# Order and pacing of two expert tables in a fused transformer kernel: where the second table begins, and how four lists of numbers share the side work

## The chip, the cores and the metric

The kernel runs on one core of a Trainium2 chip. Its engines work side by side, each through its own list of instructions in order: TensorE (PE, matmuls), VectorE (DVE), ScalarE (ACT), GpSimd (POOL) and SyncE (SP); the last three also issue DMAs, which 16 DMA engines share. The metric is the time of one execution in microseconds (us): 4077.38 us as the median of three runs (4074.62 to 4083.49).

## The reference, cut to what matters

Two transformer blocks over 512 tokens of width 1024. All that the change touches is one layer of the first block, a product-key expert layer with 16384 experts, 8 heads and the 16 best experts of each head:

```
s    = einsum('thsd,hsnd->thsn', q, sub_keys)      # scores of 2 x 128 sub-keys
sv, si = top_k(s, 16)                              # per half, then the best 16 of the sums
top, pos = top_k(sv0 + sv1, 16);  e = index of the expert;  g = softmax(top)
act  = gelu(einsum('thkd,td->thk', u_tab[e], x))   # first table, 16384 x 1024
out  = einsum('thk,thkd->td', g * act, v_tab[e])   # second table, 16384 x 1024
```

Everything is float32. The other layers (attention, a state-space mixer, cross attention, gated feed-forward layers) stay as they are.

## The kernel before, in words

A float32 product is made of three matmuls of the faster fp32r type: each operand is split into a high and a low part (`halves`: ACT writes `whi` at L119, DVE writes `wlo` at L120), and `mm3` (L167 to L169) adds high x high, high x low and low x high in PSUM. Weights come by SP in pieces of 1 MB into three buffers `wraw`, the split parts lie in three pairs of 128x1024, so the split can be at most one and a half pieces ahead of PE.

The expert layer (`experts`) splits the tokens. **384 tokens** are done densely: all 16384 experts are evaluated, and a sparse matrix of gates picks what counts.
- First table: 64 units (`unit`, L1245, counted from 1 here), each of 256 experts: 1 MB of weights, 48 matmuls with 384 columns, two Gelus (L1252) into `at`, which ACT writes to DRAM (`act_dram`, L1258). Such a group of results is called spilled.
- Gates: `select` finds the 16 best per token (DVE), `gates` (L1184) builds for 16 tokens at a time a 128x128 matrix per token out of two one-hot tiles `ga` and `gb` (DVE and ACT), multiplies them on PE (L1190), and ACT copies the result transposed into `st` (L1191) and stores it to `gate_dram` (L1218, L1223). 96 steps of four tokens each. A row of four tokens is a step of the generator `side`.
- Second table: 16 groups of 1024 experts. `weigh` (L1278) reads a group's gates `gt` (POOL, L1283) and activations `ac` (POOL, L1330), multiplies them (`wt`, L1287) and splits the product on ACT and DVE (L158, L159) into tiles `x` or `w`. `combine` (L1294) multiplies it with four pieces of the second table, each 1 MB and 48 matmuls with 384 columns. `weigh` of a group is written ahead of `combine` of the group before it.

**128 tokens** are done by gathering (`gathered`, L997): for each of 128 slots POOL gathers a row of the first table for every token (an indirect DMA of 128 rows of 4 KB, L1005) and DVE takes its dot product (L1010); 18 slots later POOL gathers a row of the second table and DVE adds it to `accg` (L1021). These 256 steps are called rows below. A row is made to wait on PE's last matmul of a unit or piece two (DVE) or four (POOL) before it (`paced`), so that it doesn't run ahead. What is left of them is issued at the start of the last group (L1298), since the sum is needed after three of its four pieces.

Numbers share the side work out. After each unit `due` grows by `DUE` = 6.5, and steps of `side` are issued until their costs have used it up; a gate step costs `GCOST` = 2.0, and steps of `gates` and of the next `select` alternate. `some(n)` adds n to a credit and issues one row per whole credit: 1.5 per unit of the first table once the rows may begin (from the seventh unit), 2 per unit that is evaluated in the second part, 2.75 per piece of the second table (`RATE`). The loop over units (L1255) goes on while side work is left, at most to 64; here side work ends with unit 62 and the count is rounded up to 64. So `first` = 16: all 16 groups are spilled and read back, in the order 0 to 15. A scheduler then orders each engine's list by when operands should be ready, so instructions can stand before others that were written earlier.

The tiles of the first part (`pa`, `pg`) give their memory to those of the second (`pb`): the first writer there waits for all that used it.

Of the kernel before, what the change touches and what calls it, by code (L numbers as in the profile page):

```python
# [21 lines left out]
P = 128  # L22
# [11 lines left out]
         + [(f"ffn_g{l}{i}", 8) for l in range(2) for i in range(2)]  # L34
         + [("mixer0_g", 8), ("mixer1_g", 8), ("subln_g", 1), ("mla_g_q", 4), ("mla_g_kv", 2), ("mla_g_qn", 1), ("mla_g_kn", 1)])
LAG, DUE = 2, 6.5
GCOST = 2.0
AHEAD, OUT_AT, EARLY = 0, 40, 2
PRE0, FILL0 = 2, 12
ON_POOL = (2, 3, 4, 5, 6, 7)  # L40
GATHERED = 128
PACE, PACE_D, AHEAD_G = 2, 4, 1
RATE = (1.5, 2, 2.75)
OHB, UGB = 1, 6
ULAG = 1
FIRST, STEP = (6, 3, 3), (1, 1, 1)
# [6 lines left out]
class Kern:  # L53
# [929 lines left out]
    def experts(self, ctx):  # L983
# [71 lines left out]
        with tc.tile_pool(name="pa", bufs=1) as sp_, ExitStack() as es:  # L1055
# [21 lines left out]
            x, xt = [], []  # L1077
# [106 lines left out]
            def gates(tt):  # L1184
# [8 lines left out]
                for tb in range(max(tt * P - G, 0) // TG, (tt * P + P - G) // TG):  # L1193
                    st = self.t(ap, [P, P, TG], "st", bufs=2)
                    for t0 in range(0, TG, 4):
                        t = tb * TG + t0
                        a = self.t(ap, [P, 4, P], "ga", bufs=LAG + 2)
                        four = lambda n: picks[n][:, t:t + 4, None].to_broadcast([P, 4, P])
                        rows4 = iota[:, None, :].to_broadcast([P, 4, P])

                        if t0 // 4 % 4 != 3:
                            nc.vector.tensor_tensor(a, rows4, four(0), op=ALU.is_equal)
                            for i in range(4):
                                nc.scalar.activation(a[:, i, :], a[:, i, :], AF.Copy, scale=picks[2][:, t + i:t + i + 1])
                        else:
                            for i in range(4):
                                nc.scalar.activation(a[:, i, :], iota, AF.Abs, bias=picks[0][:, t + i:t + i + 1], scale=-1.0)
                            for i in range(4):
                                nc.scalar.activation(a[:, i, :], a[:, i, :], AF.Relu, bias=picks[2][:, t + i:t + i + 1],
                                                     scale=picks[3][:, t + i:t + i + 1])  # L1210
                        bs = self.t(ap, [P, 4, P], "gb", bufs=LAG + 1)
                        nc.vector.tensor_tensor(bs, rows4, four(1), op=ALU.is_equal)
                        late.append((st, t0, a, bs, tb))
                        if len(late) > LAG:
                            z = late.pop(0)
                            finish(*z[:4])
                            if z[1] == TG - 4:
                                nc.scalar.dma_start(gate_d[z[4]], z[0].rearrange("p i t -> p (i t)"))  # L1218
                        yield GCOST
                for z in late:  # L1220
                    finish(*z[:4])
                    if z[1] == TG - 4:
# [29 lines left out]
                    nc.scalar.activation(out[:, i, :], ps, AF.Gelu)  # L1252

            work, due, b = side(), 0.0, 0
            while b < 64 and (b < 60 or work is not None or b % 4):  # L1255
                at = self.t(ap, [P, 2, N], "at", bufs=2)
                unit(b, at)
                nc.scalar.dma_start(act_d[b], at.rearrange("p a t -> p (a t)"))  # L1258
# [6 lines left out]
                    else:  # L1265
                        due -= c
                if room:
                    some(RATE[0])
            for _ in work or ():
                pass  # L1270
        first = b // 4
        with tc.tile_pool(name="pb", bufs=2) as ap:
# [45 lines left out]
                            if dh == 1:  # L1318
                                self.done(m)

            order, W = [*range(first, 16), *range(first)], None
            for i, c in enumerate(order):
                ac = [self.t(ap, [P, 2, 2, N], "ac", bufs=3) for _ in range(2)]
                if c >= first:
                    for b in range(4):
                        unit(c * 4 + b, ac[b // 2][:, b % 2])
                        some(RATE[1])
                else:
                    for b in range(2):
                        nc.gpsimd.dma_start(ac[b].rearrange("p b a t -> p b (a t)"), act_d[c * 4 + 2 * b:c * 4 + 2 * b + 2].rearrange("b j c -> j b c"))  # L1330
                W2 = weigh(c, lambda b: ac[b // 4][:, b % 4 // 2, b % 2, :], *((ap, "w") if i % 2 else (self.xp, "x")))
                if W is not None:
                    combine(order[i - 1], W, i == 1, False)
                W = W2
# [554 lines left out]
```

## Time and profile before

| | before |
|---|---|
| median of three runs | 4077.38 us |
| the profiled execution | 4081.56 us, span 4079.8 us |
| PE busy | 3915.7 us (96%) |
| DVE busy | 2464.4 us (60%) |
| ACT busy | 1733.6 us (42%) |
| POOL busy | 742.2 us (18%) |
| units of the first table | 618.1 (end of the first) to 1279.7 us |
| last Gelu to first matmul of the second table | 1279.7 to 1296.0 us |
| second table | 1296.0 to 1901.0 us |

The profile is one execution. PE is busy nearly all the time, so time is to be had only where it idles or runs at a low clock; a share over the whole span hides that. The views used below: busy time by stretch, with the clock that was granted to TensorE (1.00 is 2.4 GHz, 0.50 is 1.2 GHz) and the share of the DMA engines; instructions in order of time; totals of waits; groups of instructions by line; and the DMA queues.

### The profile page before, as it was taken

What the parts mean: (1) busy time and instruction counts of PE and PEld (TensorE: products, weight loads), DVE (VectorE), ACT (ScalarE), POOL (GpSimd) and SP (SyncE); (2) the same over time, 40 slices, a digit from 0 to 9 for tenths busy, and PEclk for the clock granted to TensorE, in tenths of its full rate; (3) what the DMA queues carried; (4) which work ended last, traced back from release to release, by engine and by line L of the source; (5) the groups of instructions that cost most, each with busy time, mean ns of one, the idle gap of its engine ahead of it and who ended that gap; (6) DMA issues with size and microseconds to landing.
All of it is one profiled execution on the core that took longest, in us unless ns stands there. A gap on an engine that the chain in (4) does not pass through costs nothing.

```text
span 4079.8 us, 52099 instructions
## 1 busy us (share of the span) xinstructions
PE 3915.7 (96%) x20105; PEld 3436.6 (84%) x20105; DVE 2464.4 (60%) x4683; ACT 1733.6 (42%) x3040; POOL 742.2 (18%) x706
## 2 busy tenths in 40 slices
PE   7999999999997898999999999999999999999999
PEld 6878789899987898898888778888888888888887
DVE  7666449987655787876434665743444446665443
ACT  3445434567684333333223356522332236654222
POOL 7401101122212455553000200100010001010000
PEclk8989999999998999999999999999999999999999
DMA  4204126677867999994232310323232222121222
GB/s 136 78 27 145 62 83 213 235 261 260 273 232 248 355 361 351 347 352 166 88 104 88 105 63 32 104 87 105 87 104 88 103 91 73 42 102 64 98 102 80
DMA packets 130907, 611.42 MB, mean 150 GB/s; under 512 B 22417, under 2 KB 25665, under 8 KB 90337
## 3 DMA queue, kind: packets, MB, share of 16 engines
q1 hardware_dynamic: 55296, 362.96, 25.5%
q0 software_dynamic: 48960, 187.31, 13.2%
q10 hardware_dynamic: 26400, 57.80, 3.9%
q8 instruction: 158, 2.59, 0.3%
q14 instruction: 93, 0.75, 0.1%
HBM read 553.49 MB, written 54.53 MB: 149 GB/s over the span
## 4 chain that ended last, share of the span: by engine, by line
PE 52%; DVE 5%; DMA 3%; ACT 1%; issue 1%; POOL 1%; ACTq 0%; DVEq 0%; POOLq 0%
PE ps_ffn L168 12%; PE ps_ffn L169 12%; PE ps_ffn L167 12%; DMA gt_peer<-gate_dram 2%; PE ps_mixer L168 2%; PE ps_mixer L167 2%; PE ps_mixer L169 2%; PE ps_xm L167 1%; PE ps_xm L169 1%; PE ps_xm L168 1%; PE ps_peer L169 1%; PE ps_peer L167 1%; PE ps_peer L168 1%; PE ps_mixer L1696 1%; PE ps_mixer L1549 1%
## 5 line engine op out<-in xcount | busy, mean ns | idle before, releaser
L119 ACT ACTIVATE whi_ffn<-wraw_ffn 128x1024 fp32r<-128x1024 f32 (+2 forms) x304 | 278.7, 944 | 923.6 <-PE ps_ffn L168 920.3
L167 PE MATMUL ps_peer<-xh_peer,whi_peer 128*128 128x384 f32 (+1 forms) x1664 | 582.0, 350 | 37.4 <-ACT whi_peer L119 18.1
L169 PE MATMUL ps_peer<-xh_peer,wlo_peer 128*128 128x384 f32 (+1 forms) x1664 | 576.4, 348 | 42.0 <-DVE wlo_peer L120 41.9
L168 PE MATMUL ps_peer<-xl_peer,whi_peer 128*128 128x384 f32 (+1 forms) x1664 | 574.8, 346 | 0.0
L119 ACT ACTIVATE whi_peer<-wraw_peer 128x1024 fp32r<-128x1024 f32 x272 | 285.7, 1056 | 463.3 <-PE ps_peer L168 434.7
L120 DVE TENSOR_TENSOR wlo_ffn<-wraw_ffn,whi_ffn 128x1024 fp32r<-128x1024 f32 (+2 forms) x304 | 330.9, 1090 | 180.6 <-ACT whi_ffn L119 179.9
L120 DVE TENSOR_TENSOR wlo_peer<-wraw_peer,whi_peer 128x1024 fp32r<-128x1024 f32 x272 | 329.1, 1220 | 133.1 <-ACT whi_peer L119 117.3
L169 PEld LDWEIGHTS ps_peer<-xh_peer,wlo_peer 128*128 128x128 f32 x1664 | 321.5, 193 | 54.0 <-DVE wlo_peer L120 48.5
L167 PEld LDWEIGHTS ps_peer<-xh_peer,whi_peer 128*128 128x128 f32 x1664 | 321.8, 193 | 45.7 <-ACT whi_peer L119 21.0
L331 DVE TENSOR_TENSOR g_ffn<-ps_ffn,rb_ffn 128x512 f32<-128x512 f32 x88 | 60.8, 691 | 481.0 <-PE ps_ffn L169 481.0
L168 PEld LDWEIGHTS ps_peer<-xl_peer,whi_peer 128*128 128x128 f32 x1664 | 321.5, 193 | 5.0 <-DVE xl_peer L159 0.3
L167 PE MATMUL ps_ffn<-xh_xm,whi_ffn 128*128 128x512 f32 x704 | 274.2, 390 | 0.0
L169 PE MATMUL ps_ffn<-xh_xm,wlo_ffn 128*128 128x512 f32 x704 | 273.9, 389 | 0.0
L168 PE MATMUL ps_ffn<-xl_xm,whi_ffn 128*128 128x512 f32 x704 | 273.9, 389 | 0.0
L167 PE MATMUL ps_ffn<-ah_ffn,whi_ffn 128*128 128x512 f32 x704 | 273.9, 389 | 0.0
L168 PE MATMUL ps_ffn<-al_ffn,whi_ffn 128*128 128x512 f32 x704 | 273.9, 389 | 0.0
L169 PE MATMUL ps_ffn<-ah_ffn,wlo_ffn 128*128 128x512 f32 x704 | 273.9, 389 | 0.0
L200 POOL TENSOR_TENSOR sqacc_ffn<-sqacc_ffn,sq_ffn 128x512 f32<-128x512 f32 x21 | 30.6, 1458 | 1034.2 <-ACT sq_ffn L199 1028.0
L169 PE MATMUL ps_peer<-wh_peer,wlo_peer 128*128 128x384 f32 x512 | 173.1, 340 | 18.4 <-DVE wlo_peer L120 18.4
L168 PE MATMUL ps_peer<-wl_peer,whi_peer 128*128 128x384 f32 x512 | 172.5, 337 | 0.0
L167 PE MATMUL ps_peer<-wh_peer,whi_peer 128*128 128x384 f32 x512 | 172.4, 337 | 0.0
L1005 POOL DMA_INDIRECT ug_peer<-in_peer_v_rows_dram,idx_peer x94 | 140.5, 1495 | 154.4 <-DVE accg_peer L1021 117.5
(761 smaller groups left out, 9236.7 us busy)
## 6 DMA issues: line engine op xcount, KB each, us to landing
wraw_ffn<-in_ffn_gu_dram SPq DMA_DIRECT2D x88, 1024.0 KB
wraw_peer<-in_peer_u_dram SPq DMA_DIRECT2D x64, 1024.0 KB
wraw_peer<-in_peer_v_dram SPq DMA_DIRECT2D x64, 1024.0 KB
wraw_ffn<-in_ffn_dn_dram SPq DMA_DIRECT2D x64, 704.0 KB
act_dram<-at_peer ACTq DMA_DIRECT2D x64, 384.0 KB
gate_dram<-st_peer ACTq DMA_DIRECT2D x24, 1024.0 KB
ac_peer<-act_dram POOLq DMA_DIRECT2D x32, 768.0 KB
gt_peer<-gate_dram POOLq DMA_DIRECT2D x32, 768.0 KB
```

What stands on the lines that cost most here:

```text
L119: nc.scalar.activation(hi[:, :m], raw, AF.Copy)
L120: nc.vector.tensor_sub(lo[:, :m], raw, hi[:, :m].bitcast(F32))
L167: nc.tensor.matmul(ps, a[0], b[0], start=first, stop=False)
L168: nc.tensor.matmul(ps, a[0], b[1], start=False, stop=False)
L169: nc.tensor.matmul(ps, a[1], b[0], start=False, stop=last)
L200: nc.gpsimd.tensor_add(acc[:, :n], acc[:, :n], sq[:, :n])
L331: nc.vector.tensor_mul(g, pg, rb)
L1005: nc.gpsimd.indirect_dma_start(out=u, out_offset=None, in_=A[table], in_offset=bass.IndirectOffsetOnAxis(ap=idx[:, s:s + 1], axis=0))
L1549: nc.tensor.matmul(ps[:, (jj - j) * P:n], lhs, l, start=False, stop=False, skip_group_check=True)
L1696: nc.tensor.matmul(S[it][:, :n], hT[0, h][:, i * P:n], hT[1, h][:, :n], start=True, stop=True)
```

## The change

`GCOST` becomes a list by 128-token block, the first loop ends with unit 60 unless side work is left, and the order of the second part begins with group 0. Side work now ends with unit 59, the loop ends at 60, `first` is 15, and the order is 0, 15, 1, 2, ... 14: group 0 is read and weighed (`read`, `weigh`), then units 61 to 64 are evaluated into `ac` in SBUF without a way through DRAM (`evaluate`), then group 0 is combined. Rows: 0.9 per unit up to the 27th, 2.6 per unit from the 28th on and in `evaluate`, 2.2 per piece. The tiles for the weighed groups change places (`w` for the even ones, `x` for the odd ones), since `x` is still read by the units.

```diff
-GCOST = 2.0
+GCOST = (1.5, 1.5, 1.5, 2.4)
-RATE = (1.5, 2, 2.75)
+RATE = (0.9, 2.6, 2.2)
-                        yield GCOST
+                        yield GCOST[tt]
-            while b < 64 and (b < 60 or work is not None or b % 4):
+            while b < 60 or b < 64 and work is not None or b % 4:
-                    some(RATE[0])
+                    some(RATE[0 if b < 28 else 1])
+            def read(c):
+                ac = [self.t(ap, [P, 2, 2, N], "ac", bufs=3) for _ in range(2)]
+                for b in range(2):
+                    nc.gpsimd.dma_start(ac[b].rearrange("p b a t -> p b (a t)"), act_d[c * 4 + 2 * b:c * 4 + 2 * b + 2].rearrange("b j c -> j b c"))
+                return ac
+            def evaluate(c):
+                ac = [self.t(ap, [P, 2, 2, N], "ac", bufs=3) for _ in range(2)]
+                for b in range(4):
+                    unit(c * 4 + b, ac[b // 2][:, b % 2])
+                    some(RATE[1])
+                return ac
-            order, W = [*range(first, 16), *range(first)], None
+            order, W = [0, *range(first, 16), *range(1, first)], None
             for i, c in enumerate(order):
...
+                ac = evaluate(c) if c >= first else read(c)
-                W2 = weigh(c, lambda b: ac[b // 4][:, b % 4 // 2, b % 2, :], *((ap, "w") if i % 2 else (self.xp, "x")))
+                W2 = weigh(c, lambda b: ac[b // 4][:, b % 4 // 2, b % 2, :], *((self.xp, "x") if i % 2 else (ap, "w")))
```

DVE where the first table ends, before. `wlo` of `wraw` 11690 and 11757 are the units 63 and 64, that of 11947 and 12014 pieces of the second table; `wt` is the weighing of group 0, which waits for `gt`.

```order
L120 TENSOR_TENSOR wlo_peer_11693<-wraw_peer_11690,whi_peer_11692 128x1024
L1021 SCALAR_TENSOR_TENSOR accg_peer_4356<-sc_peer_11686,act_peer_4359,accg_peer_4356 128x1024
L120 TENSOR_TENSOR wlo_peer_11697<-wraw_peer_11690,whi_peer_11696 128x1024
L120 TENSOR_TENSOR wlo_peer_11760<-wraw_peer_11757,whi_peer_11759 128x1024
L120 TENSOR_TENSOR wlo_peer_11764<-wraw_peer_11757,whi_peer_11763 128x1024
L1010 SCALAR_TENSOR_TENSOR sc_peer_11753,hid_peer_4358<-sc_peer_11753,xg_peer_4355 128x1024
L1021 SCALAR_TENSOR_TENSOR accg_peer_4356<-sc_peer_11820,act_peer_4359,accg_peer_4356 128x1024
L120 TENSOR_TENSOR wlo_peer_11950<-wraw_peer_11947,whi_peer_11949 128x1024
L120 TENSOR_TENSOR wlo_peer_11954<-wraw_peer_11947,whi_peer_11953 128x1024
L1010 SCALAR_TENSOR_TENSOR sc_peer_11823,hid_peer_4358<-sc_peer_11823,xg_peer_4355 128x1024
L120 TENSOR_TENSOR wlo_peer_12014<-wraw_peer_12011,whi_peer_12013 128x1024
L1287 TENSOR_TENSOR wt_peer_11837<-ac_peer_11831,gt_peer_11835 128x384
```

The same place now. `wraw` 11684, 11755, 11823 and 11896 are the units 61 to 64.

```order
L120 TENSOR_TENSOR wlo_peer_11687<-wraw_peer_11684,whi_peer_11686 128x1024
L120 TENSOR_TENSOR wlo_peer_11691<-wraw_peer_11684,whi_peer_11690 128x1024
L1021 SCALAR_TENSOR_TENSOR accg_peer_4356<-sc_peer_11618,act_peer_4359,accg_peer_4356 128x1024
L120 TENSOR_TENSOR wlo_peer_11758<-wraw_peer_11755,whi_peer_11757 128x1024
L120 TENSOR_TENSOR wlo_peer_11762<-wraw_peer_11755,whi_peer_11761 128x1024
L120 TENSOR_TENSOR wlo_peer_11826<-wraw_peer_11823,whi_peer_11825 128x1024
L120 TENSOR_TENSOR wlo_peer_11830<-wraw_peer_11823,whi_peer_11829 128x1024
L1287 TENSOR_TENSOR wt_peer_11632<-ac_peer_11626,gt_peer_11630 128x384
L1287 TENSOR_TENSOR wt_peer_11638<-ac_peer_11626,gt_peer_11630 128x384
L159 TENSOR_TENSOR wl_peer_11635<-wt_peer_11632,wh_peer_11634 128x384
L1287 TENSOR_TENSOR wt_peer_11644<-ac_peer_11626,gt_peer_11630 128x384
L120 TENSOR_TENSOR wlo_peer_11899<-wraw_peer_11896,whi_peer_11898 128x1024
```

Before, all units have been split when the first weighing waits. Now three whole units that PE has still to do stand split ahead of it, and the fourth in the midst of it; behind the weighing stand five dot products and five additions of rows, and only then the first split of the second table.

ACT late in the first table, before: the end of what stands between the two splits of unit 60's weights (`wraw` 11363).

```order
L1252 ACTIVATE at_peer_11249<-ps_peer_11286 128x384
L1209 ACTIVATE ga_peer_11327<-ga_peer_11327,pick_peer_5180,pick_peer_5181 128x128
L1258 DMA act_dram<-at_peer_11249 128x768
L1191 ACTIVATE st_peer_11211<-ps_peer_11321 128x4x128
L1209 ACTIVATE ga_peer_11327<-ga_peer_11327,pick_peer_5180,pick_peer_5181 128x128 x2
L1191 ACTIVATE st_peer_11211<-ps_peer_11338 128x4x128
L1204 ACTIVATE ga_peer_11345<-ga_peer_11345,pick_peer_5180 128x128 x4
L1191 ACTIVATE st_peer_11211<-ps_peer_11353 128x4x128
L119 ACTIVATE whi_peer_11369<-wraw_peer_11363 128x1024
```

And now, between those of unit 54 (`wraw` 10893):

```order
L1252 ACTIVATE at_peer_10789<-ps_peer_10826 128x384
L1204 ACTIVATE ga_peer_10854<-ga_peer_10854,pick_peer_5180 128x128
L1258 DMA act_dram<-at_peer_10789 128x768
L1204 ACTIVATE ga_peer_10854<-ga_peer_10854,pick_peer_5180 128x128
L1191 ACTIVATE st_peer_10649<-ps_peer_10862 128x4x128
L1204 ACTIVATE ga_peer_10868<-ga_peer_10868,pick_peer_5180 128x128 x4
L1191 ACTIVATE st_peer_10649<-ps_peer_10876 128x4x128
L119 ACTIVATE whi_peer_10899<-wraw_peer_10893 128x1024
```

Gate steps still come in heaps between two splits. Counted in copies `st` from a unit's first split to that of the next unit, the heaps were 9 (unit 53), 3 and 6 (units 56 and 57) and 10 (unit 60); they are now 9 (unit 48) and 8 each (units 51, 54 and 57). Earlier in the table the largest was 6 (unit 34) and is now 7 (units 19 and 32).

DVE in the second table, before: three pieces, `wraw` 14012, 14079 and 14202.

```order
L120 TENSOR_TENSOR wlo_peer_14015<-wraw_peer_14012,whi_peer_14014 128x1024
L120 TENSOR_TENSOR wlo_peer_14019<-wraw_peer_14012,whi_peer_14018 128x1024
L1021 SCALAR_TENSOR_TENSOR accg_peer_4356<-ug_peer_14009,act_peer_4359,accg_peer_4356 128x1024
L1010 SCALAR_TENSOR_TENSOR ug_peer_14070,hid_peer_4358<-ug_peer_14070,xg_peer_4355 128x1024
L1021 SCALAR_TENSOR_TENSOR accg_peer_4356<-ug_peer_14073,act_peer_4359,accg_peer_4356 128x1024
L120 TENSOR_TENSOR wlo_peer_14082<-wraw_peer_14079,whi_peer_14081 128x1024
L120 TENSOR_TENSOR wlo_peer_14086<-wraw_peer_14079,whi_peer_14085 128x1024
L1010 SCALAR_TENSOR_TENSOR ug_peer_14076,hid_peer_4358<-ug_peer_14076,xg_peer_4355 128x1024
L1021 SCALAR_TENSOR_TENSOR accg_peer_4356<-ug_peer_14137,act_peer_4359,accg_peer_4356 128x1024
L1010 SCALAR_TENSOR_TENSOR ug_peer_14140,hid_peer_4358<-ug_peer_14140,xg_peer_4355 128x1024
L120 TENSOR_TENSOR wlo_peer_14205<-wraw_peer_14202,whi_peer_14204 128x1024
```

And now, in the same part of a group (`wraw` 14044 and 14110):

```order
L1021 SCALAR_TENSOR_TENSOR accg_peer_4356<-ug_peer_13977,act_peer_4359,accg_peer_4356 128x1024
L1010 SCALAR_TENSOR_TENSOR ug_peer_14038,hid_peer_4358<-ug_peer_14038,xg_peer_4355 128x1024
L120 TENSOR_TENSOR wlo_peer_14047<-wraw_peer_14044,whi_peer_14046 128x1024
L120 TENSOR_TENSOR wlo_peer_14051<-wraw_peer_14044,whi_peer_14050 128x1024
L1021 SCALAR_TENSOR_TENSOR accg_peer_4356<-ug_peer_14041,act_peer_4359,accg_peer_4356 128x1024
L1010 SCALAR_TENSOR_TENSOR ug_peer_14102,hid_peer_4358<-ug_peer_14102,xg_peer_4355 128x1024
L120 TENSOR_TENSOR wlo_peer_14113<-wraw_peer_14110,whi_peer_14112 128x1024
L1015 TENSOR_TENSOR act_peer_4359<-act_peer_4359,g_peer_4360 128x16
L159 TENSOR_TENSOR wl_peer_14183<-wt_peer_14180,wh_peer_14182 128x384
```

Three rows stood between the splits of two pieces, and two stand there now; the weighing of the next group is spread over more pieces than before.

## Rows read from the trace of the kernel before

**Rows 1.** Busy time by stretch (us), instructions in brackets; granted clock, DMA share.

```profile
618.10:888.10 270.00, 254.20 (x1485) 251.30 (x1484) 265.93 (x876) 148.79 (x275) 51.58 (x36) 0.97 0.68 234
888.10:1124.40 236.30, 234.58 (x1460) 233.87 (x1459) 157.41 (x202) 165.48 (x328) 54.21 (x36) 1.00 0.79 272
1124.40:1279.70 155.30, 139.68 (x856) 136.64 (x855) 86.01 (x109) 115.74 (x244) 23.52 (x15) 0.95 0.65 227
1279.70:1296.00 16.30, 0.00 (x0) 0.00 (x0) 2.60 (x5) 1.00 (x4) 5.12 (x5) 0.62 0.75 245
1296.00:1901.00 605.00, 558.75 (x3081) 550.90 (x3082) 478.71 (x646) 197.83 (x267) 309.89 (x231) 0.96 0.90 335
```

**Rows 2.** Instructions in time, ACT: the last Gelu of two successive units.

```profile
626.40 0.47 ACT L1252 ACTIVATE at_peer<-ps_peer 128x384 f32<-128x384 f32 x1
...
634.72 0.47 ACT L1252 ACTIVATE at_peer<-ps_peer 128x384 f32<-128x384 f32 x1
```

**Rows 3.** Groups by line, 618.1 to 1279.7 us: gate matmuls on PE.

```profile
L1190 PE MATMUL ps_peer<-ga_peer,gb_peer 128*128 128x128 f32 x768 | 93.8, 275 | 0.0
```

**Rows 4.** Busy time by stretch, as Rows 1: three late units.

```profile
1138.10:1154.20 16.10, 13.01 (x73) 12.49 (x73) 7.31 (x9) 10.87 (x24) 3.42 (x3) 0.89 0.60 221
...
1188.60:1208.10 19.50, 14.99 (x82) 14.33 (x81) 11.25 (x14) 15.02 (x33) 3.40 (x3) 0.82 0.59 204
...
1230.20:1250.20 20.00, 14.05 (x81) 13.39 (x81) 10.57 (x13) 15.05 (x32) 2.35 (x2) 0.83 0.47 173
```

**Rows 5.** Instructions in time, all engines, between the two tables.

```profile
1279.68 0.47 ACT L1252 ACTIVATE at_peer<-ps_peer 128x384 f32<-128x384 f32 x1
...
1280.18 0.33 ACTq L1258 DMA_DIRECT2D act_dram<-at_peer  x1
1284.17 1.55 POOL L1330 DMA_DIRECT2D ac_peer<-act_dram  x2 [30.92 <-DMA act_dram<-at_peer]
1287.20 2.87 POOL L1283 DMA_DIRECT2D gt_peer<-gate_dram  x2 [1.48 <-issue]
...
1294.86 1.03 DVE L1287 TENSOR_TENSOR wt_peer<-ac_peer,gt_peer 128x384 f32<-128x384 f32 x2 [13.59 <-DMA gt_peer<-gate_dram]
```

**Rows 6.** Waits of DVE, 1290 to 1900 us: total us, times, longest.

```profile
DVE wt_peer L1287 <- DMA gt_peer<-gate_dram: 75.0, 14, 13.6
```

**Rows 7.** DMA queues, 1290 to 1840 us: packets, MB, share of 16 engines; issues.

```profile
q0 software_dynamic: 34033, 132.68, 66.3%
q1 hardware_dynamic: 8064, 58.72, 27.4%
...
wraw_peer<-in_peer_v_dram SPq DMA_DIRECT2D x56, 1024.0 KB
...
ug_peer<-in_peer_v_rows_dram,idx_peer POOLq DMA_INDIRECT x86
ug_peer<-in_peer_u_rows_dram,idx_peer POOLq DMA_INDIRECT x75
```

**Rows 8.** Groups by line, 1290 to 1840 us, DVE: busy us, mean ns.

```profile
L120 DVE TENSOR_TENSOR wlo_peer<-wraw_peer,whi_peer 128x1024 fp32r<-128x1024 f32 x113 | 136.3, 1220 | 15.1 <-ACT whi_peer L119 15.0
...
L1021 DVE SCALAR_TENSOR_TENSOR accg_peer<-ug_peer,act_peer,accg_peer 128x1024 f32<-128x1024 f32 x80 | 102.5, 1281 | 18.1 <-PE ps_peer L169 15.1 <-DMA ug_peer<-in_peer_v_rows_dram,idx_peer 3.0
...
L1010 DVE SCALAR_TENSOR_TENSOR ug_peer<-ug_peer,xg_peer 128x1024 f32<-128x1024 f32 x75 | 91.4, 1219 | 10.9 <-PE ps_peer L169 10.5 <-DMA ug_peer<-in_peer_u_rows_dram,idx_peer 0.3
...
L1287 DVE TENSOR_TENSOR wt_peer<-ac_peer,gt_peer 128x384 f32<-128x384 f32 x128 | 65.7, 552 | 75.1 <-DMA gt_peer<-gate_dram 75.0
...
L159 DVE TENSOR_TENSOR wl_peer<-wt_peer,wh_peer 128x384 fp32r<-128x384 f32 x64 | 33.4, 553 | 1.1 <-ACT wh_peer L158 0.2
```

**Rows 9.** Waits of DVE, 618 to 1280 us.

```profile
DVE accg_peer L1021 <- PE ps_peer L169: 46.5, 15, 8.8
DVE sc_peer L1010 <- PE ps_peer L169: 45.8, 16, 5.9
```

**Rows 10.** Busy time by stretch, as Rows 1: 20 us of the second table.

```profile
1700.00:1720.00 20.00, 17.74 (x102) 17.42 (x101) 14.46 (x23) 7.01 (x11) 9.54 (x9) 1.00 1.02 399
```

More of the change, by code (lines that the diff above doesn't have):

```diff
@@ L1319, in combine @@
                                 self.done(m)
-            order, W = [*range(first, 16), *range(first)], None
-            for i, c in enumerate(order):
[L1323 to L1330, printed above, removed]
-                W2 = weigh(c, lambda b: ac[b // 4][:, b % 4 // 2, b % 2, :], *((ap, "w") if i % 2 else (self.xp, "x")))
+            def read(c):
[10 more added lines that the diff above has]
+            order, W = [0, *range(first, 16), *range(1, first)], None
+            for i, c in enumerate(order):
+                ac = evaluate(c) if c >= first else read(c)
+                W2 = weigh(c, lambda b: ac[b // 4][:, b % 4 // 2, b % 2, :], *((self.xp, "x") if i % 2 else (ap, "w")))
                 if W is not None:
```

## The prediction

> **What bounds the kernel now.** I read the busy time by stretch first, and what PE lacks in each of them. Nearly all of the span is PE at work, and none of that is touched: the same 64 units and 64 pieces are computed. What can change is lost time, which I count in a stretch as PE's idle time plus what a granted clock below 1.00 costs (one minus the clock, times the stretch) [rows 1]:
> - 618.1 to 888.1 us: 15.8 idle + 0.03 x 270.0 = 23.9 us. DVE is busy 265.9 of 270.0: here it is the bound.
> - 888.1 to 1124.4: 1.7 us. PE is the bound, with DVE at 0.67 and the DMA engines at 0.79.
> - 1124.4 to 1279.7: 15.6 + 0.05 x 155.3 = 23.4 us.
> - 1279.7 to 1296.0: all 16.3 us.
> - 1296.0 to 1901.0: a piece has as many matmuls of the same shape as a unit, and two successive units end 634.72 - 626.40 = 8.32 us apart [rows 2], so 64 pieces need 532.5 us; 605.0 - 532.5 = 72.5 us are lost. Idle time and clock give 46.3 + 24.2 = 70.5, so the two ways of counting agree.
>
> Together 137.8 us. (By unit lengths the first three would be 661.6 - 63 x 8.32 - 93.8 of gate matmuls [rows 3] = 43.6 instead of 49.0; I stay with the larger.) The change can win at most this, some 3.4%.
>
> Then I asked what loses it. **Second table:** DVE waits 75.0 us in 14 waits for gates to be read from DRAM [rows 6], and the splits of weights stand behind these waits in its list. The reads are late since the DMA engines are full: the two queues take 66.3 + 27.4 = 93.7% of 550 us, which is 515 us of transfers for 56 pieces [rows 7], while PE needs 56 x 8.32 = 466. **Between the tables:** a chain. Last Gelu at 1279.68, its results land and POOL asks for `ac` at 1284.17 and for `gt` at 1287.20, DVE begins to weigh at 1294.86 [rows 5]. Call the first of these times T: gates are there at T + 15.2. **Late first table:** the loss sits in three units, with 4.9 (3.1 idle + 1.8 clock), 8.0 and 9.3 us by the same count; ACT is busy 15.0 of 19.5 us in the second [rows 4]. They follow the heaps of 9, of 3 + 6 and of 10 gate copies in ACT's list.
>
> **The change part by part.**
>
> Rows. Of 256, the first loop issued 58 x 1.5 = 87; now 21 x 0.9 + 33 x 2.6 = 104.7, and 10.4 in the four units that follow. A piece issues 2.2 instead of 2.75.
>
> *Second table, 72.5 to 25 us.* In 56 pieces 31 rows fall away. Queue 0 took 0.663 x 550 = 365 us for 132.68 MB; 161 rows of 0.524 MB are 84.4 MB of it, so 1.44 us each [rows 7]. 31 x 1.44 = 45 us, and 515 becomes 470, level with PE's 466. DVE per four pieces: 8 splits at 1.22, 11 rows at about 1.29 (the dot's accumulator read of some 0.08 counted in), 8 + 8 instructions of 0.55 for weighing [rows 8] are 32.8 us of PE's 33.3; now 8.8 rows, 29.9 us, and the order shows one row less in a gap between pieces. POOL can hold six row buffers: these are now 2.7 pieces of work instead of 2.2, so a gate read that stands behind them in its list goes out some 4 us earlier in PE's time, against a mean wait of 75.0 / 14 = 5.4 us. Bounds: 0, and 72.5 as before. The excess of transfers over PE was 515 - 466 = 49 us in 56 pieces, 56 in 64, and the other 16 were heaps; I take 25: those 16, an excess of 4 and 5 for bursts.
>
> A page bears on this. The Trainium skill, "DMA: Bandwidth & Descriptors" (Specifications), gives some 358 GB/s as a core's limit from HBM. By it the 191.4 MB less 16.2 would need an estimated 489 us rather than 470, and the loss would be about 45 instead of 25. The stretch at 399 GB/s [rows 10] does not agree with a hard limit there, and the mean of 335 [rows 1] lies below it, so I keep the queues' own times.
>
> *Between the tables, 16.3 to 11 us.* With T now the end of unit 60, PE has units 61 to 64 to do, until T + 33.3, and three of them are split ahead of the weighing. So the chain to T + 15.2 is hidden. What is late next is DVE: from T + 15.2 it has 16 weighing instructions (8.8), two splits of unit 64 (2.4) and then the ten rows of the four units (12.9), all in front of the first split of the second table, which ends at 15.2 + 8.8 + 2.4 + 12.9 + 1.2 = T + 40.5. PE waits 7.2 us, and a low clock costs some 3.4 as in the late units. Bounds: 0 if the gates or the rows are quicker, 24 if the gates, now read beside rows and weights, come 13 us later. That four groups' results needn't go through DRAM (1.5 MB each way) I cost at nothing: the transfers lie beside PE's work.
>
> *First table to 1124.4, 25.6 to 35 us.* Until the selects are done DVE is the bound, and its list up to unit 28 is as long as before: fewer rows (0.9 instead of 1.5), but gate steps that come sooner. I leave 26 for that. From unit 28 rows are 2.6 a unit and heaps of 7 copies stand at units 19 and 32, where the largest was 6; I take 4.5 for each, the price of the cheapest late heap. Bounds 15 and 50.
>
> *Late first table, 23.4 to 16 us.* Four heaps, of 9, 8, 8 and 8. Heaps of 9 and 10 cost 4.9 and 9.3 [rows 4], so 8 should cost less than 4.9: I take 4.9 + 3 x 3, and 2 of small gaps. Bounds 7 and 39 (four at 9.3 and the same 2).
>
> *End, 0 to 2 us.* Ten rows instead of five are left for the last group; they stand as heaps of five additions, 8.8 us with the splits, beside pieces of 8.32. Bounds 0 and 10.
>
> Sum: 35 + 16 + 11 + 25 + 2 = 89 us are lost instead of 137.8, a gain of 49. From the profiled execution, 4081.6 - 49 = 4032.6; it was 4.2 us above the median of the runs, so 4028.
>
> **The rivals.**
> 1. *The second table keeps its loss* because the gate reads are late by themselves, whatever the rows do: they are asked for 7.0 us after T and need another 7.7 in a stretch where no rows run [rows 5]. Against it: 45 us of transfers fall away. Then 35 + 16 + 11 + 72.5 + 2 = 136.5 are lost, a gain of 1: 4076 us, no change.
> 2. *Slower: rows hold DVE in the first table.* DVE's list is in order and a row waits for PE's end of a unit; before, 92.3 us of such waits [rows 9] for 87 rows, 1.06 us each, cost nothing from 888.1 on, since DVE had 243 us of work in 392 [rows 1]. Now 83 rows fall on 32 units there, with about 271 us of work (243, 29 rows more at 1.3, four units' splits less) in PE's 333 (391.6 less the 25.1 lost and four units). At 2.1 us a row the waits are 174 and DVE's time 445, 112 more than PE's: lost are 26 + 112 + 11 + 25 + 2 = 176, 38 more than before: 4116. It decides from 1.6 us a row, where DVE's time passes PE's by the 74 us that would eat the whole gain; at today's 1.06 it costs no more than my two terms. Against it: these waits show a DVE that is early, and a fuller DVE is less so.
> 3. *More gain:* heaps and bursts cost next to nothing: 26 + 7 + 3 + 10 + 0 = 46 lost: 3986.
>
> **How the numbers follow.** Forecast 0.64, with its own range of 4000 to 4058; rival 1 0.13, rival 2 0.08, rival 3 0.15. The range for 8 in 10 runs from 3985 to 4068: it takes in most of rival 3 and stops short of rivals 1 and 2. About 0.2% (8 us) is what a measurement of this kernel can tell from no change. Faster by more: 0.64, 0.15 and a little of rival 1, 0.82; within it 0.09; slower 0.09.
>
> **What would show it.** In the profile after: DVE's total wait for gate reads in the second table well below 75 us, and a DMA share below 0.90 at a shorter stretch of some 557 us; no PE gap after unit 60, but one of several us before the first piece; the late gaps of PE after heaps of eight copies, below 5 us each; from unit 28 to 48 PE's idle time below 10 us. The prediction is wrong if the second table stays above 590 us, or if PE waits for splits behind rows throughout units 28 to 60.

## The result, and the profile after

The changed kernel takes 4026.38 us (median of four runs, 4024.42 to 4027.49) where the kernel before took 4080.38 beside it (four runs; the first three gave the 4077.38 above): a ratio of 0.9869, with an interval of 0.9852 to 0.9886. That is 54 us or 1.3% less, 2 us from the forecast of 4028.

Busy time by stretch after, with the columns of [rows 1] (us; busy us and instructions of PE, weight loads, DVE, ACT, POOL; granted clock; DMA share; GB/s). The stretches are units 2 to 28, 29 to 48, 49 to 60, then 61 to 64 as far as PE had work, its wait for the second table, and that table:

```profile
619.00:889.00 270.00, 256.47 (x1499) 252.31 (x1498) 257.31 (x868) 152.08 (x283) 36.14 (x25) 0.97 0.62 214
889.00:1104.50 215.50, 208.13 (x1290) 206.47 (x1289) 165.36 (x216) 158.81 (x325) 71.55 (x55) 0.98 0.88 315
1104.50:1257.80 153.30, 137.67 (x827) 135.01 (x826) 97.76 (x123) 108.27 (x222) 34.70 (x26) 0.94 0.72 259
1257.80:1292.00 34.20, 34.20 (x196) 33.49 (x194) 18.26 (x27) 13.89 (x24) 11.58 (x12) 1.00 0.87 317
1292.00:1304.10 12.10, 0.06 (x2) 0.01 (x1) 10.55 (x15) 1.54 (x3) 10.27 (x9) 0.62 0.85 275
1304.10:1845.70 541.60, 535.96 (x3073) 534.04 (x3074) 443.73 (x593) 191.43 (x259) 288.84 (x210) 1.00 0.93 345
```

Counted as in the prediction, PE's idle time and what the clock costs, the first three rows lose 21.6, 11.7 and 24.8 us, where [rows 1] had 23.9, 1.7 and 23.4 in stretches that end at other units. The second table takes 541.6 us instead of 605.0. Its DMA share rose from 0.90 to 0.93 and its granted clock from 0.96 to 1.00.

DVE's waits for gates, 1250 to 1846 us, against the 75.0 us in 14 waits of [rows 6] (total us, times, longest):

```profile
DVE wt_peer L1287 <- DMA gt_peer<-gate_dram: 22.1, 5, 7.1
```

PE's waits from 1104 to 1846 us. 12.0 of the first line's 16.8 us are the one wait ahead of the second table; nearly all of the second line is the four heaps of gate copies in units 49 to 60:

```profile
PE ps_peer L169 <- DVE wlo_peer L120: 16.8, 4, 12.0
PE ps_peer L167 <- ACT whi_peer L119: 16.3, 7, 5.0
```

DVE's list between the tables, answering to [rows 5] (start us, us, instruction; in brackets the idle time before it and what ended it):

```profile
1278.78 1.03 DVE L1287 TENSOR_TENSOR wt_peer<-ac_peer,gt_peer 128x384 f32<-128x384 f32 x2 [7.11 <-DMA gt_peer<-gate_dram]
...
1289.44 1.02 DVE L159 TENSOR_TENSOR wl_peer<-wt_peer,wh_peer 128x384 fp32r<-128x384 f32 x2
1290.38 1.28 DVE L1021 SCALAR_TENSOR_TENSOR accg_peer<-ug_peer,act_peer,accg_peer 128x1024 f32<-128x1024 f32 x1
...
1301.62 1.28 DVE L1021 SCALAR_TENSOR_TENSOR accg_peer<-ug_peer,act_peer,accg_peer 128x1024 f32<-128x1024 f32 x1 [0.60 <-DMA ug_peer<-in_peer_v_rows_dram,idx_peer]
1302.82 2.35 DVE L120 TENSOR_TENSOR wlo_peer<-wraw_peer,whi_peer 128x1024 fp32r<-128x1024 f32 x2
```

Unit 60 ends at 1257.8, the gates are there 21 us later, the weighing is done at 1290.4, and then DVE works through rows for 12.4 us before it makes the first split that PE needs.

### The profile page after: what moved, and what is told of

It is laid out like the page before. It is cut to its first block, busy times and chain, and to the rows that moved or that the text cites. A ratio compares the mean times of both kernels' runs of the same rounds, so it can differ in the third digit from the quotient of the medians.

```text
span 4025.5 us, 52157 instructions
## 1 busy us (share of the span) xinstructions
PE 3903.0 (97%) x20105; PEld 3426.6 (85%) x20105; DVE 2466.5 (61%) x4683; ACT 1730.9 (43%) x3040; POOL 745.9 (19%) x704
## 3 DMA queue, kind: packets, MB, share of 16 engines
q1 hardware_dynamic: 55296, 362.96, 25.6%
q0 software_dynamic: 48672, 185.73, 13.1%
## 4 chain that ended last, share of the span: by engine, by line
PE 80%; DVE 11%; ACT 3%; DMA 2%; issue 1%; POOL 1%; SPq 0%; ACTq 0%; DVEq 0%; POOLq 0%
PE ps_ffn L168 12%; PE ps_ffn L167 12%; PE ps_ffn L169 12%; PE ps_peer L169 7%; PE ps_peer L167 7%; PE ps_peer L168 7%; PE ps_mixer L168 2%; PE ps_mixer L167 2%; PE ps_mixer L169 2%; DVE wlo_peer L120 2%; PE ps_peer L1190 1%; DMA gt_peer<-gate_dram 1%; PE ps_xm L167 1%; PE ps_mem L167 1%; PE ps_xm L169 1%
## 5 line engine op out<-in xcount | busy, mean ns | idle before, releaser
L169 PE MATMUL ps_peer<-xh_peer,wlo_peer 128*128 128x384 f32 (+1 forms) x1664 | 570.9, 344 | 12.5 <-DVE wlo_peer L120 12.2
L167 PEld LDWEIGHTS ps_peer<-xh_peer,whi_peer 128*128 128x128 f32 x1664 | 318.2, 191 | 38.1 <-ACT whi_peer L119 30.9
L169 PEld LDWEIGHTS ps_peer<-xh_peer,wlo_peer 128*128 128x128 f32 x1664 | 317.5, 191 | 22.4 <-DVE wlo_peer L120 16.8
L1005 POOL DMA_INDIRECT ug_peer<-in_peer_v_rows_dram,idx_peer x85 | 135.9, 1598 | 128.0 <-DVE accg_peer L1021 59.2
```

The costliest lines, as they stand in the source:

```text
L167: nc.tensor.matmul(ps, a[0], b[0], start=first, stop=False)
L169: nc.tensor.matmul(ps, a[1], b[0], start=False, stop=last)
L1005: nc.gpsimd.indirect_dma_start(out=u, out_offset=None, in_=A[table], in_offset=bass.IndirectOffsetOnAxis(ap=idx[:, s:s + 1], axis=0))
```

## The experiments

All runs are counted by one ledger from their own profile, in us. Table 1: from the end of unit 1 to the end of the last spilled unit, less 8.32 for each unit and the 93.8 of [rows 3]. Between: from there to the first piece, less 8.32 for each unit evaluated in that time. Second: the second table less 532.5. "Gates" is what the profile puts down to gate reads of DVE's waits, in all. Each ratio is to the kernel before as it ran beside that run, so runs are compared by ratios and not by medians alone.

| run | median us | ratio to before, 95% | table 1 | between | second | gates |
|---|---|---|---|---|---|---|
| before | 4080.38 | | 43.6 | 16.3 | 72.5 | 75.0 |
| after | 4026.38 | 0.9852 to 0.9886 | 54.1 | 13.0 | 9.1 | 22.1 |
| e1 rates only | 4029.39 | 0.9848 to 0.9881 | 42.4 | 15.1 | 26.3 | 24.3 |
| e2 order only | 4070.97 | 0.9963 to 0.9988 | 64.3 | -0.1 | 58.9 | 66.1 |
| e3 before, short DVE rows | 4024.98 | 0.9838 to 0.9871 | 35.2 | 16.1 | 23.4 | 80.5 |
| e5 after, paced copies | 4027.99 | 0.9854 to 0.9887 | 54.1 | 11.0 | 11.3 | 18.0 |
| e6 before, half rows | 4164.03 | 1.0187 to 1.0221 | 102.2 | 15.6 | 94.3 | 15.1 |
| e7 evaluated group first | 4033.10 | 0.9862 to 0.9895 | 55.1 | 5.9 | 23.2 | 38.1 |
| e8 no rows between | 4015.50 | 0.9824 to 0.9857 | 66.2 | 1.6 | 1.1 | 16.5 |
| e9 before, gates on SP | 4030.73 | 0.9863 to 0.9901 | 43.6 | 12.2 | 24.7 | 8.7 |
| e10 after, four buffers | 4032.37 | 0.9865 to 0.9900 | 53.6 | 6.2 | 24.5 | 26.0 |
| e11 smaller heaps | 3997.17 | 0.9779 to 0.9810 | 45.4 | 4.2 | 3.3 | 13.9 |

Two waits ahead of a first weighing stand beside the last column: 12.4 us in e1 that the profile puts down to nothing, and 9.5 us in e9 for activations (`ac`).

**e1 and e2: the two halves of the change.**

```diff
e1  -RATE = (1.5, 2, 2.75)
    +RATE = (0.9, 2.6, 2.2)
    -                    some(RATE[0])
    +                    some(RATE[0 if b < 28 else 1])
e2  all the rest of the change, with RATE = (1.5, 2, 2.75)
```

> The kernel before with the changed row rates alone (0.9 up to the 27th unit, 2.6 after it, 2.2 per piece); gate costs and the order of groups stay. In the changed kernel the second table needs 541.6 us, 9 over the 532.5 of its 64 pieces, where it was 72 over. Theory 1 (the rate): fewer rows per piece are the whole of it, so the second table needs 540 to 555 us here, the gap of 16 us between the tables stays, and the time is 4025 to 4045 us. Theory 2 (the order): beginning with group 0 and evaluating group 15 in the second part is what smooths it, so the second table still loses 50 us or more and the time is 4065 to 4085.

> The changed kernel with the old row rates (1.5, 2 and 2.75): only the gate costs and the order of groups are changed. Theory 1 (the rate): the second table loses 55 to 75 us as before, and the time is 4060 to 4080 us. Theory 2 (the order): the second table loses under 25 us, and the time is 4015 to 4035. Both: the gap between the tables is about 12 us, since ten rows (8 here) stand on VectorE behind the weighing; late heaps of eight gate copies cost what they cost in the changed kernel (25 us for four) if ScalarE's heap sets the price, and 10 to 15 if the rows among them do.

The rates alone bring the whole gain: e1's interval is nearly that of the changed kernel (its second table takes 558.8 us, 4 more than theory 1 gave). The order and the gate costs alone bring 0.25%. In e2 they win 30 us from the end of the first table on, and lose 21 of that in the first, by heaps of gate copies: units 32, 36 and 40, which lost next to nothing before, lose 4.4, 5.8 and 6.6 us, and units 49, 52, 55 and 58 lose 4.9, 7.8, 6.5 and 7.5, where the three late units of before lost 20. The -0.1 between the tables hides one stop: PE begins the first piece, waits 4.6 us for a split at 1305.25, and the table counts that in the second table. About 12 us were expected there; seven rows stand ahead of that split, not ten. On top of the rates they lose 12 us in the first table (54.1 against 42.4) and win 17 in the second.

**e3: DVE's part of the rows cut, the bytes kept.**

```diff
-scalar_tensor_tensor(u, u, 1.0, xg, ...)
+scalar_tensor_tensor(u[:, :256], u[:, :256], 1.0, xg[:, :256], ...)   # the sum likewise
```

> The kernel before, but VectorE takes only the first 256 of 1024 columns of each gathered row (the gathers stay whole, so the values of 128 tokens are left out in part). A row costs VectorE some 0.4 instead of 1.25 us; transfers are unchanged. Theory A (transfers): the second table keeps 50 us or more of its loss of 72, since 515 us of transfers for 56 pieces stay, and gate reads are waited for as before. Theory B (VectorE's list, its load and its heaps): the loss falls below 25 us. Either way the first table gains 5 to 20 us up to 890 us, where VectorE is the bound.

The second table, busy time by stretch:

```profile
1289.10:1845.00 555.90, 540.35 (x3081) 535.97 (x3082) 347.28 (x646) 196.75 (x267) 273.35 (x231) 0.99 0.94 364
```

All rows are still fetched, at 364 GB/s and in 49 us less than before. So transfers alone did not set the 605 us. The waits for gates did not shrink (80.5 us), but DVE now makes up for them, with 347 us of work instead of 479: late gates cost PE time where DVE's list leaves no slack behind them.

**e4 and e5: more transfers in the changed kernel.**

```diff
+nc.gpsimd.dma_start(more[next(extra)], A["peer_v_rows"][0:72])       # in each piece
+tc.add_manual_dep(..., pace[-4].name, ...)                           # e5 alone
```

> The changed kernel with a DRAM-to-DRAM copy of 0.295 MB added per piece of the second table (64 copies, issued by GpSimd; nothing reads them), about what 0.55 rows were; VectorE's list is nearly the same. Theory A (transfers): the second table loses 45 to 75 us again, and the time is 4065 to 4090. Theory B (VectorE's list): it loses under 25 us, and the time is 4025 to 4040.

e4 told nothing. Since its copies waited for nothing, all 64 ran at the kernel's start (17.6 to 124 us); it took 4042.28 us, and its second table lost 11.3 us with no more bytes than the changed kernel's. e5 mends that.

> The changed kernel with 64 more copies of 0.29 MB from DRAM to DRAM on POOL's queue, one in each piece of the second table; each is tied to the first matmul of a piece some four before it, so that they are spread over the table, where in the run before they all ran at the start. At the 1.44 us of queue time that a row of 0.52 MB took, 0.29 MB are 0.8 us and the 64 copies some 51 us, about as much as the change took away. Theory A (transfers set the loss of the second table, as the prediction argued): its time goes from 541.6 back to 575 to 605 us, a loss of 45 to 70. Theory B (DVE's list in order sets it, and transfers hide beside it): 540 to 555 us, a loss below 22, with a DMA share of 0.93 or more. Whole kernel: A 4060 to 4090 us, B 4025 to 4040.

The second table of e5:

```profile
1300.30:1844.10 543.80, 537.38 (x3072) 534.59 (x3072) 437.40 (x588) 189.83 (x253) 301.68 (x262) 0.99 0.98 377
```

The DMA engines are busy 0.98 of the time and move 205 MB, where the kernel before moved 202 (377 GB/s over 543.8 us, 335 over 605.0), and the table loses 11.3 us instead of 9.1. The added copies go from DRAM to DRAM; the rows and weights are those of the changed kernel. With e3 this settles it against the transfers: the prediction's 515 against 470 us was not what decided.

**e6: half the bytes of each row in the kernel before.**

```diff
-indirect_dma_start(out=u, ..., in_=A[table], ...)
+indirect_dma_start(out=u[:, :512], ..., in_=A[table].rearrange("e (a b) -> (e a) b", a=2), ...)
```

> The kernel before with half the bytes in every gathered row: only 512 of its 1024 columns are fetched, so the 128 tokens' own result is not the reference's. DVE does as much as before, in two instructions of 512 columns where there was one of 1024. In the second table some 161 rows of 0.72 us less queue time make the transfers about 110 us shorter. It is the counterpart of the run in which DVE's part of the rows was cut and the bytes were kept. Theory A (transfers): the second table falls from a loss of 72.5 to below 25 us, the DMA share to about 0.75, DVE's waits for gates from 75 to below 30. Theory B (DVE's list): the loss stays at 50 to 75 us whatever the DMA share falls to; the waits for gates may fall, since less is ahead of them. Whole kernel: A 4015 to 4040, B 4060 to 4085.

Neither theory's number came. DVE's waits in the second table:

```profile
DVE ug_peer L1011 <- DMA ug_peer<-in_peer_u_rows_dram,idx_peer: 56.2, 28, 4.6
DVE accg_peer L1024 <- DMA ug_peer<-in_peer_v_rows_dram,idx_peer: 54.7, 40, 4.3
```

The DMA share fell to 0.74 and waits for gates to 15 us, but DVE now waits 111 us for rows. The two instructions of a row stand apart in DVE's list, other work between them, and DVE has more to do (496 us instead of 479). That a row buffer is held longer by it and POOL asks for the next row later is my guess; it was not measured. It is no clean test; it shows that neither a DMA share of 0.74 nor short waits for gates keep the table from losing 94 us.

**What stands in POOL's list.** POOL in the kernel before, 1418 to 1443 us (its gathers of rows are L1005):

```profile
1418.00 0.94 POOL L1005 DMA_INDIRECT ug_peer<-in_peer_v_rows_dram,idx_peer  x1 [0.30 <-issue]
1429.40 1.01 POOL L1005 DMA_INDIRECT ug_peer<-in_peer_u_rows_dram,idx_peer  x1 [10.46 <-DVE ug_peer L1010]
1432.47 2.62 POOL L1005 DMA_INDIRECT ug_peer<-in_peer_v_rows_dram,idx_peer  x1 [2.06 <-DVE accg_peer L1021]
...
1439.85 1.54 POOL L1330 DMA_DIRECT2D ac_peer<-act_dram  x2
1441.34 2.90 POOL L1283 DMA_DIRECT2D gt_peer<-gate_dram  x2
```

DVE and PE in the same time:

```profile
1427.90 1.22 DVE L1010 SCALAR_TENSOR_TENSOR ug_peer<-ug_peer,xg_peer 128x1024 f32<-128x1024 f32 x1
...
1450.46 1.22 DVE L120 TENSOR_TENSOR wlo_peer<-wraw_peer,whi_peer 128x1024 fp32r<-128x1024 f32 x1
1458.09 1.03 DVE L1287 TENSOR_TENSOR wt_peer<-ac_peer,gt_peer 128x384 f32<-128x384 f32 x2 [6.41 <-DMA gt_peer<-gate_dram]
...
1466.27 1.02 DVE L1287 TENSOR_TENSOR wt_peer<-ac_peer,gt_peer 128x384 f32<-128x384 f32 x2
...
1471.64 2.35 DVE L120 TENSOR_TENSOR wlo_peer<-wraw_peer,whi_peer 128x1024 fp32r<-128x1024 f32 x2
```

```profile
1472.91 0.69 PE L169 MATMUL ps_peer<-xh_peer,wlo_peer 128*128 128x384 f32 x1 [5.60 <-DVE wlo_peer L120]
```

It is a ring. DVE's dot product at 1427.90 stands within the weighing of one group; POOL waits 10.46 us for the buffer that it frees; the next gates stand behind this gather and go out at 1441.34; DVE waits 6.41 us for them, a split stands behind the wait and behind 11.5 us more of weighing and four rows, and PE stops for 5.60 us. The wait and the work behind it make the stop together. In the kernel before POOL waited 199 us for DVE to free row buffers between 1300 and 1840 us, in the changed one 110 us:

```profile
POOL ug_peer L1005 <- DVE accg_peer L1021: 106.7, 27, 12.9
POOL ug_peer L1005 <- DVE ug_peer L1010: 92.5, 23, 11.5
```

```profile
POOL ug_peer L1005 <- PE ps_peer L169: 66.0, 22, 5.3
POOL ug_peer L1005 <- DVE accg_peer L1021: 58.1, 32, 9.4
POOL ug_peer L1005 <- DVE ug_peer L1010: 51.7, 23, 8.1
```

Behind it 66 us are waits for PE (`paced`): POOL is now ahead, held back on purpose. That a gate read is late because of what stands ahead of it in POOL's list is theory C below.

**e9 and e10: POOL's list by itself.**

```diff
e9   -nc.gpsimd.dma_start(gt.rearrange(...), gate_d[...])   # in the kernel before
     +nc.sync.dma_start(gt.rearrange(...), gate_d[...])
e10  -OHB, UGB = 1, 6                                       # in the changed kernel
     +OHB, UGB = 1, 4
```

> The kernel before with one word changed: gates are read by SP's queue and no longer by POOL's, where in the kernel before they stand behind gathers of rows that wait for DVE to free a row buffer (199 us of such waits of POOL in 23 + 27 times, in the second table). Rows, bytes and DVE's list stay as they were. The last runs speak against transfers (more bytes in the changed kernel's second table, at a DMA share of 0.98, cost it 2 us). Theory C (a gate read is late because it stands behind rows in POOL's list, and then holds the splits behind it in DVE's): DVE's waits for gates fall from 75 to below 25 us, the loss of the second table from 72.5 to 10 to 35, and the whole kernel takes 4015 to 4045 us. Theory A (the transfers are too long): the waits stay above 60 us and the kernel within 10 us of 4081. A third way: the weights are issued on SP too, a gate read that waits for its buffer holds them, and PE then waits for weights: 4080 to 4150.

The second table of e9, and DVE's waits for gates in 1282 to 1850 us:

```profile
1293.30:1850.50 557.20, 542.17 (x3082) 538.12 (x3082) 477.31 (x646) 195.16 (x267) 275.55 (x199) 0.99 0.99 364
```

```profile
DVE wt_peer L1287 <- DMA gt_peer<-gate_dram: 8.7, 2, 6.4
```

One word brings 48 of the 72.5 us: the same 646 DVE instructions and 477 us of DVE work, the same rows, DMA engines busier than ever (0.99). All three numbers of theory C came, and neither rival's. The reads themselves are no quicker: those issued at 1407.22 and 1415.86 us land 17.0 and 13.6 us later, that of the ring took 16.8. They are asked for sooner: the first read of a group goes out 95 us ahead of PE's first matmul with that group, where it was 50 in the kernel before and 80 in the changed one (means of the third to fifteenth group, from the traces). One stop of PE, of 7.2 us until 1323.8, comes after the 6.42 us for which DVE waited for early gates.

But DVE's list did not stay as it was, as the expectation had it: the scheduler ordered it anew. In the ring a group's weighing stood from 1458.09 to 1467 us with one split in it; in e9 it stretches over 27 us with five splits in it:

```profile
1454.19 1.02 DVE L1287 TENSOR_TENSOR wt_peer<-ac_peer,gt_peer 128x384 f32<-128x384 f32 x2
...
1468.01 1.23 DVE L120 TENSOR_TENSOR wlo_peer<-wraw_peer,whi_peer 128x1024 fp32r<-128x1024 f32 x1 [0.48 <-ACT whi_peer L119]
...
1479.97 1.02 DVE L1287 TENSOR_TENSOR wt_peer<-ac_peer,gt_peer 128x384 f32<-128x384 f32 x2
```

On average 4.6 splits stand within a group's weighing in e9, 4.4 in the changed kernel and 1.4 in the kernel before. So e9 shows that the place of the gate reads costs the 48 us, with the order of DVE's list that follows from it; it does not tell the earlier reads from the new order, and no run holds DVE's order fixed. Nor are the two the only way: in e5 reads go out 40 us ahead and 1.5 splits stand within the weighing, and with a lighter list of DVE (437 us) the waits are 18.0 us and the loss 11.3.

> The changed kernel with four row buffers instead of six in the second table, and nothing else. POOL can then hold fewer rows ahead of DVE, and a gate read that stands behind rows in its list waits for DVE more often. Theory C (POOL's list): DVE's waits for gates rise from 22 us to 45 or more, and the loss of the second table from 9 to 25 to 70 us; whole kernel 4042 to 4090. Theory B (only the amount of work in DVE's list counts): waits and loss within 6 us of the changed kernel's, whole kernel 4020 to 4035.

The loss rose to 24.5 us, just short of what theory C gave, and for another reason than it gave: the waits for gates hardly rose (26.0), while POOL waited 176 us for buffers and DVE 24.6 us for rows. With four buffers the rows themselves come late. Theory C was not confirmed by this run, and its time lies in theory B's range.

**e7 and e8: what makes the wait between the tables.**

```diff
e7  -order, W = [0, *range(first, 16), *range(1, first)], None
    +order, W = [*range(first, 16), *range(first)], None
e8  -RATE = (0.9, 2.6, 2.2)
    +RATE = (0.9, 2.9, 2.2)
    -                    some(RATE[1])                       # in evaluate
```

> The changed kernel with one line changed: the second table begins with the group that was evaluated last (15) and not with group 0, whose results are read back. So the first weighing has to wait for the Gelu of unit 64 and not only for gates. Theory A (which group comes first counts, as the prediction's chain says): between the tables 16 to 22 us are lost instead of 13.0; whole kernel 4029 to 4036. Theory B (the ten rows in front of the first split of the second table hold PE, whichever group is first): 11 to 14 us lost there, whole kernel within 3 us of the changed one.

Both theories missed. Between the tables e7 loses less (5.9), not more: two splits stand right behind the first two weighings, at 1294.32, with the rows ahead of the weighing or behind the splits. PE waits no longer for a split there but 3.3 and 1.9 us for the weighed products, whose gates DVE had waited for 5.0 us. It gives that back in the second table (23.2, with 38.1 us of waits for gates). Why the later gates are late was not tested; that group 0 first lets POOL ask for a group ahead of need is a guess.

> The changed kernel without the ten or eleven rows that are issued in units 61 to 64, and 2.9 rows a unit instead of 2.6 from unit 28 to 60, so that as many rows are done by then. In the changed kernel the first split of the second table ended at 1304.0, after ten rows of about 2.5 us that stand in front of it in DVE's list; the weighing had ended at 1290.4. Theory A (these rows make the wait): the splits follow the weighing, PE loses 0 to 4 us between the tables instead of 13.0; units 28 to 60 lose up to 5 us more; whole kernel 4014 to 4023. Theory B (gates read late at 1278.8 or the splits' own weights set it): 10 to 13 us stay, whole kernel 4024 to 4032.

Between the tables 1.6 us are left, and the second table now loses 1.1:

```profile
1264.80:1299.70 34.90, 34.90 (x204) 34.90 (x203) 21.34 (x32) 15.85 (x28) 14.91 (x12) 1.00 0.89 311
1299.70:1833.30 533.60, 531.83 (x3067) 530.75 (x3067) 440.08 (x586) 190.85 (x258) 286.25 (x207) 1.00 0.94 346
```

So the ten rows made the wait (each of some 1.25 us, not 2.5 as the expectation says): ten ahead of the first split cost a stop of 12.0 us, seven 4.6 (e2), none next to nothing. The first table took 12 us more where up to 5 were expected; the gate copies fell into other units when the rows moved there: unit 40 now loses 6.5 us, and units 52, 55 and 58 together lose 23.8 instead of 19.0.

**e11: smaller heaps.**

```diff
-LAG, DUE = 2, 6.5
-GCOST = (1.5, 1.5, 1.5, 2.4)
+LAG, DUE = 2, 7.0
+GCOST = (1.6, 1.9, 1.9, 2.8)                               # and e8's edits
```

> The kernel without rows between the tables, with gates paced anew: DUE 7.0 for 6.5, and costs of (1.6, 1.9, 1.9, 2.8) for (1.5, 1.5, 1.5, 2.4). By the order of ACT's list its heaps of gate copies from unit 28 on are one of 7, then 8, 5, 7, 5 and 8, where the run before had two of 7 at 32 and 35, another 7 at 39, then 9, 8, 8 and 8. There units with a heap of 7 lost 4.3 to 6.5 us and those of 8 and 9 lost 4.9 to 8.1 each. If a heap is priced by its size: 3 x 6.5 for those of 7 and 8 late in the table, 4 for the one at 31, 2 for each of 5, some 28 us from unit 28 on instead of 40; whole kernel 4000 to 4010 us. If a unit pays for the number of heaps and not for their size, or earlier selects cost DVE what ACT wins: 4012 to 4022.

3997.17 us beats both kernels, by 2.1% and (by the ratio of the two ratios) 0.8%, and is 3 us below the range expected. By unit lengths units 29 to 60 lose 27 us instead of e8's 46: behind the two heaps of 5 nothing is lost, so small heaps cost next to nothing. Among heaps of 7 to 9 size does not set the price (9 copies cost 4.9 us in unit 49 of e8, 8 copies 8.1 in unit 58); units 2 to 28 lose 21 instead of 20, so the earlier selects cost DVE next to nothing. Those of e8 and e11 that lose most still stand behind heaps: 49, 52, 55 and 58 there (4.9 to 8.1 us), 32, 49, 54 and 59 here (6.1 to 8.0).

## Why the prediction was right, and where it was not

The sum was 89 us of lost time; it is 81 by the prediction's own count. The total was near by luck: one reason was wrong, and several sizes missed in opposite directions. Step by step:

- **Second table, 72.5 to 25: 9.1 measured.** Right in direction, under-sized in its gain by 16 us, and its reason was wrong. The failed step is "The reads are late since the DMA engines are full", with its 515 against 470 us. e5 filled the DMA engines again and lost 2 us more; e9 took away no bytes and won 48 us. What decided, as far as the runs show it, stood in the same paragraph as asides: that a gate read stands behind rows for which POOL has no buffer (put at 4 us sooner with the change; it was 31), and that DVE's list was full (32.8 of PE's 33.3 us; e3, which shortens it, wins 49 with the gates as late as before). Fewer rows ease both, and how much each gives in the change itself stays open. Of the 63 us won, 46 come by the rates alone (e1), the rest only with the new order.
- **DMA share below 0.90: wrong, 0.93,** for the same reason. The 45 us of loss that the prediction had estimated from the 358 GB/s of the Trainium skill, "DMA: Bandwidth & Descriptors" (Specifications), did not come. The Trainium skill, "HBM Reference" (Specifications (TRN2)), says that a core that streams alone measures well above its share of 358 GB/s; the 377 GB/s over 544 us in e5 lie above it too.
- **Rival 1** (the gate reads are late by themselves, whatever the rows do) did not come: the second table lost 9.1 us, not 72.5.
- **Between the tables, 16.3 to 11: 13.0 measured.** The mechanism held as written: ten rows ahead of the first split, one stop of 12.0 us and no other after unit 60. The gates came 5.8 us later than the T + 15.2 assumed; the 3.4 us for a low clock hardly show there, since the clock of 0.62 falls on time in which PE stands; the rest was right. e8 shows that without the rows there is no stop.
- **First table to 1124.4, 25.6 to 35: 33.3 measured** (21.6 + 11.7). Near by luck again: up to unit 28 the sum had 26 and 4.5 for the heap at unit 19, 9 too much; from there to unit 48 it had 4.5 for the heap at unit 32, 7 too little. Unit 32 lost 4.2 us as priced, but unit 35, behind a heap of 4 copies that the sum left out, lost 5.7.
- **Late first table, 23.4 to 16: 24.8 measured.** Mis-sized. I priced a heap of 8 below 4.9, the price of one heap of 9, and passed over the 8.0 us behind the heaps of 3 and 6 in the same rows. Units 49, 52, 55 and 58, busy time by stretch:

```profile
1104.50:1120.50 16.00, 13.11 (x74) 12.60 (x73) 11.13 (x14) 10.39 (x20) 4.08 (x4) 0.89 0.67 216
1142.00:1158.10 16.10, 13.29 (x76) 12.78 (x75) 10.13 (x12) 10.45 (x21) 4.22 (x4) 0.89 0.66 223
1178.70:1196.80 18.10, 13.10 (x75) 12.44 (x74) 11.63 (x14) 13.51 (x27) 3.29 (x3) 0.91 0.59 208
1217.40:1236.70 19.30, 14.47 (x80) 13.81 (x79) 12.84 (x15) 13.67 (x28) 2.80 (x2) 0.82 0.60 213
```

  Less 8.32 and the unit's gate matmuls they lose 4.9, 4.8, 6.8 and 7.4 us. The idle gaps alone, which I had named as the sign (below 5 each), are 2.6, 2.5, 5.0 and 4.8, one of them just at that bound; smaller gaps and a clock of 0.82 to 0.91 make up the rest. Four heaps of 8 and 9 cost 24 us, where the late heaps of before cost 20.
- **End: 1 us** (2179.8 behind the second table instead of 2178.8).
- **Rival 2** (rows hold DVE in the first table) did not come: units 29 to 48 lose PE 7.4 us of idle time at 0.88 of DMA share.

So the two largest errors have opposite signs: 16 us too little hoped for in the second table, 9 too much of the late heaps.

## What to carry to other kernels

A full DMA share beside a late read does not say that the read waits for bandwidth: read what the engine that issues it was doing before, since a read queued behind gathers that wait for a buffer is as late as that buffer. Give a small read that gates a critical list a queue without such gathers before cutting the bulk traffic: here that brought 48 us with all bytes kept. And count what stands ahead of the first instruction that the bound engine needs: ten rows there cost 12 us, seven 4.6. When one word is changed, compare the order of every engine's list before calling the run a test of that word.

## What was not expected of the hardware

DMA engines busy 0.98 to 0.99 of 544 and 557 us (e5, e9) left PE at a granted clock of 0.99 with 6.4 and 15.0 us of idle time: at 364 to 377 GB/s the loads of weights still came early enough for PE. In e9 not for ACT: the loads stand behind gate reads in SP's list there (13 us pass from the first of a pair to the next load), and ACT waited 69.6 us for weights in the second table, where in e5 it waited for none. PE hardly stopped for it; its waits of 1293 to 1850 us hold 13.1 us at the table's start and 7.2 until 1323.8, and little else:

```profile
PE ps_peer L167 <- ACT xh_peer L158: 14.7, 2, 13.1
PE ps_peer L169 <- DVE wlo_peer L120: 13.0, 6, 7.2
```

```profile
ACT whi_peer L119 <- DMA wraw_peer<-in_peer_v_dram: 69.6, 10, 9.7
```

```profile
1407.22 13.30 SPq L1283 DMA_DIRECT2D gt_peer<-gate_dram  x2
1420.62 16.73 SPq L111 DMA_DIRECT2D wraw_peer<-in_peer_v_dram  x4
```
